# Six edits of one layer kernel: the last tile's splits put first, M6 ahead of M4, adaLN beside V, x loaded first, the last pair kept in SBUF

## The chip, the cores and the metric

The kernel runs on one core of a Trainium2 chip. The metric is the time of one execution on the device in microseconds (us). The engines of the core work side by side and wait for each other by semaphores: PE (TensorE, matrix products), DVE (VectorE), ACT (ScalarE), POOL (GpSimd) and SP (SyncE, which here issues the DMA transfers). PE's clock has two levels, 1.2 and 2.4 GHz; the profile gives the granted clock of a stretch as a share of the higher one.

## The reference, cut to what matters

The kernel computes one hybrid decoder layer over 1024 tokens of 1024 channels.

```
mod = silu(c) @ w_ada + b_ada                     # shift1, scale1, gate1, shift2, scale2, gate2
h = rmsnorm(x, norm1_w) * (1 + scale1) + shift1
proj = h @ w_in                                   # attention q k v, indexer, retention q k v, gates
qr = rotate(qr); kr = rotate(kr) * 128 ** -0.5    # retention keys and queries (4 heads of 128)
att = dsa_attention(...)                          # top-256 by an indexer's score
ret = silu(gr) * groupnorm(retention(qr, kr, vr))
merged = sigmoid(ga) * (att @ w_attn_proj) + sigmoid(gb) * (ret @ w_ret_proj)
x = x + gate1 * (merged @ w_out)
h2 = rmsnorm(x, norm2_w) * (1 + scale2) + shift2
x = x + gate2 * ((silu(h2 @ w_ffn_gate) * (h2 @ w_ffn_up)) @ w_ffn_down)
out = rmsnorm(x, final_norm_w)
```

## The kernel before

Every float32 operand of a large product is **split** into a high and a low part that PE takes (names ending in `hi` and `lo`): ACT copies the operand to `hi`, and POOL or DVE subtracts, `lo = operand - hi`. A product is then three matmuls, hi·hi, hi·lo and lo·hi. `lo_engine` names the engine of the subtraction; `turns_after(a, b)` only sets the order of two instructions on one engine. A scheduler orders the rest, and each engine works its list in order.

The stages, in order of time:

- **Start (0 to 80 us).** SP loads five small rows (`rows`: c, b_ada and norm weights), then the first block of w_ada (`load_wa(0)`), then four tiles of x. For each of eight blocks j, DVE sums `acc` over eight slices of w_ada (L293, L295), PE transposes it, and DVE makes the two columns `modc` (L300, L301). `make_h` (L270) transposes x, ACT writes `hT_hi` and `hx` from PSUM (L277, two instructions), and `lo_engine` makes `hT_lo` (L278: POOL for the first half of the tokens, DVE for the second). Then PE multiplies block j.
- **Rotated retention queries and keys (QR; 231 to 281 us for the first head pair, hp = 0).** Per tile t of eight: PE projects, ACT copies (`qk`, L650), POOL rotates in seven instructions (L657 to L663: `rra`, `rrb`, `rq`, `kk`), PE transposes `rq` and `kk` (L666, L667). Meanwhile DVE runs count passes of the top-k search (L463, `eq`) and steps of `mod_work` (L529, `macc`: the other four sixths of adaLN, 32 steps, each with a load `mw` of 512 KB). A step is called once per t.
- **V and retention (V_R)**, with one step of `mod_work` per t for hp = 0; then attention.
- **Gate region (500 to 715 us).** Products by Strassen's scheme: `Stream` takes 256 columns of a weight in seven products M1 to M7 of half size, whose weight operands are sums of the blocks b11, b12, b21, b22 (`factor`, L762 makes `lo`), and whose results DVE adds up (`add`, L821). The token side (`h11`, `h21`, `S1` to `S4`) is made from `sums` (L625, L638, L639). `seq` is the order of the products, `behind(i)` what else is issued behind product i.
- **FFN start (1110 to 1135 us).** The normalised h2 of the last tile group is transposed, scaled (L1404), split into `hc` (`put_combo`, L1294 and L1295), and the first two streams begin: M1 and M5 early, then M2, M4, M6, M3, M7.
- **FFN streams (1200 to 1540 us).** 22 streams: 11 pairs p of gate and up columns. After a pair, its activations (`act_d`, seven per pair) and the sums of its w_ffn_down blocks (`dw_d`, L1502) go to DRAM.
- **Down product (from 1560 us).** For each of M1, M5, M6, M3, M7, M4 and each p, `down_slot` loads an operand (`draw`, from `act_d`, `dw_d` or w_ffn_down), ACT makes the high part (`dslot`, L1603), DVE or POOL the low one (L1604), and PE multiplies (L1621 to L1623).

Of the kernel before, what the change touches and what calls it, by code (L numbers as in the profile page):

```python
# [43 lines left out]
def tile_hybrid_layer(ctx: ExitStack, tc: tile.TileContext, x, c, w_ada, b_ada, norm1_w, w_in,  # L44
# [202 lines left out]
    rows = start.tile([80, P], F32, name="rows")  # L247
    nc.sync.dma_start(out=rows[0:8, :], in_=c.rearrange("o (k p) -> (o k) p", p=P))
# [4 lines left out]
    load_wa(0)  # L253
    for t in range(4):
        load_x(t)
# [14 lines left out]
    def make_h(j, hf, lo_engine):  # L270
# [5 lines left out]
        for to in (hi, hx):  # L276
            nc.scalar.activation(to, tp, AF.Identity, scale=modc[:, j, 2:3], bias=modc[:, j, 0:1])  # L277
# [7 lines left out]
    def start_mod(j):  # L285
        if j:
            load_wa(j)
# [218 lines left out]
    mod_ins = [None]  # L506

    def mod_work():
# [12 lines left out]
        for n, (m, k) in enumerate(steps):  # L521
# [10 lines left out]
            mod_ins[0] = ins  # L532
# [108 lines left out]
    for hp in range(2):  # L641
# [3 lines left out]
        for t in range(NT):  # L645
# [71 lines left out]
        for t in range(NT + 1):  # L717
# [42 lines left out]
    def split_block(src, hi, lo, eng=None):  # L760
        ins = nc.scalar.activation(hi, src, AF.Copy)  # L761
        (eng or nc.gpsimd).tensor_sub(lo, src, f32(hi))  # L762
        return ins

    class Stream:
# [5 lines left out]
        def __init__(self, env, w, c0):  # L771
# [3 lines left out]
            self.next = None  # L775

        def open(self):
            if self.blocks:
                return
            for kh in range(2):  # L780
# [13 lines left out]
        def factor(self, m):  # L794
# [3 lines left out]
            elif m == "M4":  # L798
                src = self.t2
                nc.vector.tensor_sub(src, b["21"], src)  # L800
            else:
                src = four(self.env.tmp())
                x, y = {"M5": ("12", "11"), "M6": ("22", None), "M7": ("22", "12")}[m]
                if m == "M6" and "M5" in self.early:
                    self.t1 = src
                    nc.vector.tensor_sub(src, b["12"], b["11"])
                nc.vector.tensor_sub(src, b[x], b[y] if y else self.t1)  # L807
# [5 lines left out]
            self.split = split_block(src, hi, lo, self.env.lo_engine)  # L813
# [70 lines left out]
    class GateEnv:  # L884
# [23 lines left out]

        def store(self, st, dst, src):
# [5 lines left out]
        def use(self, st, c):  # L915
# [99 lines left out]
    seq = [(st, m) for m in ORDER for st in flow[:2]]  # L1015
# [6 lines left out]
    def behind(i):  # L1022
        n, m = 2 + (i - 14) // 7, seq[i][1]
        if i == 6:
            genv.lo_engine = None
        if i >= 15 and (i - 15) % 6 == 0 and 22 + (i - 15) // 6 < len(passes) - 1:
            turns_after(passes[22 + (i - 15) // 6], genv.added)
        if 14 <= i < n_mid:
# [3 lines left out]
            if n in (8, 9) and m == "M1":  # L1032
# [723 lines left out]
```

## Time and profile before

| quantity | value |
|---|---|
| median of 3 runs | 1771.59 us (1771.57 to 1774.38) |
| profiled execution, its own time | 1770.31 us |
| its span | 1768.4 us |
| mean granted clock of PE | 0.991 |
| busy share PE, DVE, POOL, ACT | 96%, 69%, 50%, 43% |
| moved by DMA | 266.48 MB, 151 GB/s mean |

The span is the time from the first to the last instruction that the profile shows; the profiled execution took 1.9 us more than that, and 1.3 us less than the median. The stretches named in this document are us from the span's start. A granted clock under 1 means that PE ran at its lower level for part of the stretch.

### The profile page before, as it was taken

What the parts mean: (1) busy time and instruction counts of PE and PEld (TensorE: products, weight loads), DVE (VectorE), ACT (ScalarE), POOL (GpSimd) and SP (SyncE); (2) the same over time, 40 slices, a digit from 0 to 9 for tenths busy, and PEclk for the clock granted to TensorE, in tenths of its full rate; (3) what the DMA queues carried; (4) which work ended last, traced back from release to release, by engine and by line L of the source; (5) the groups of instructions that cost most, each with busy time, mean ns of one, the idle gap of its engine ahead of it and who ended that gap; (6) DMA issues with size and microseconds to landing.
All of it is one profiled execution on the core that took longest, in us unless ns stands there. A gap on an engine that the chain in (4) does not pass through costs nothing. (4 is left out here: it accounts for less than half of the span.)

```text
span 1768.4 us, 24625 instructions
## 1 busy us (share of the span) xinstructions
PE 1696.3 (96%) x8266; PEld 1393.6 (79%) x8266; DVE 1216.7 (69%) x2099; ACT 757.2 (43%) x1469; POOL 882.4 (50%) x873
## 2 busy tenths in 40 slices
PE   5899989999999999999999999899999999999998
PEld 4797768888878887788777888688787778787887
DVE  7529793888998687574675747865756565686665
ACT  3625533333544444430676146533333333444444
POOL 3563275683544678430355631054544445556564
PEclk9999999999999999999999999999999999999999
DMA  9535452512333355964843720134444444597762
GB/s 276 161 99 169 149 162 62 149 39 57 117 90 131 112 172 176 291 182 146 196 116 136 244 98 1 54 107 165 158 156 160 137 150 143 203 320 247 209 183 107
DMA packets 182654, 266.48 MB, mean 151 GB/s; under 512 B 13872, under 2 KB 111616, under 8 KB 180096
## 3 DMA queue, kind: packets, MB, share of 16 engines
q1 hardware_dynamic: 182528, 264.91, 48.1%
q8 instruction: 65, 1.06, 0.3%
q14 instruction: 61, 0.50, 0.1%
HBM read 195.39 MB, written 69.47 MB: 150 GB/s over the span
## 5 line engine op out<-in xcount | busy, mean ns | idle before, releaser
L80 POOL TENSOR_TENSOR wlo<-wraw,whi 128x512 fp32r<-128x512 f32 (+2 forms) x116 | 147.0, 1279 | 105.3 <-ACT whi L77 86.3
L463 DVE TENSOR_SCALAR_CACHE_REDUCE eq<-score,cand 128x384 uint8<-128x384 f32 (+2 forms) x192 | 180.5, 940 | 3.6
L762 POOL TENSOR_TENSOR flo<-tmp,fhi 128x512 fp32r<-128x512 f32 x79 | 107.1, 1356 | 139.7 <-ACT fhi L761 111.8
L121 PE MATMUL mm<-whi,hT_hi 128*128 128x512 f32 (+1 forms) x432 | 159.8, 376 | 3.8 <-ACT qk L650 1.8
L124 PE MATMUL mm<-whi,hT_lo 128*128 128x512 f32 (+1 forms) x432 | 161.5, 376 | 0.0
L123 PE MATMUL mm<-wlo,hT_hi 128*128 128x512 f32 (+1 forms) x432 | 160.3, 374 | 0.0
L838 PE MATMUL ya<-hc,fhi 128*128 128x512 f32 x344 | 134.6, 392 | 2.3 <-DVE c L821 1.4
L1604 DVE TENSOR_TENSOR dslot<-draw,dslot 128x512 fp32r<-128x512 f32 x88 | 94.7, 1107 | 58.4 <-ACT dslot L1603 54.2
L1603 ACT ACTIVATE dslot<-draw 128x512 fp32r<-128x512 f32 x154 | 90.4, 626 | 102.9 <-DMA draw<-dw_d 23.4
L840 PE MATMUL ya<-hc,fhi 128*128 128x512 f32 x344 | 133.9, 389 | 0.0
L842 PE MATMUL ya<-hc,flo 128*128 128x512 f32 x344 | 132.4, 389 | 0.0
L1604 POOL TENSOR_TENSOR dslot<-draw,dslot 128x512 fp32r<-128x512 f32 x66 | 98.0, 1498 | 65.4 <-ACT dslot L1603 61.7
L762 POOL TENSOR_TENSOR flo<-raws,fhi 128x512 fp32r<-128x512 f32 x60 | 82.1, 1369 | 92.7 <-ACT fhi L761 64.2
L77 ACT ACTIVATE whi<-wraw 128x512 fp32r<-128x512 f32 (+2 forms) x116 | 67.0, 590 | 112.0 <-DMA wraw<-in_w_in_dram 46.4
L840 PE MATMUL yb<-hc,fhi 128*128 128x512 f32 x256 | 100.6, 393 | 6.1 <-DVE hc L1295 6.1
L842 PE MATMUL yb<-hc,flo 128*128 128x512 f32 x256 | 100.7, 394 | 3.2 <-POOL flo L762 3.2
L761 ACT ACTIVATE fhi<-tmp 128x512 fp32r<-128x512 f32 x84 | 53.0, 631 | 113.1 <-PE ya L840 61.4
L838 PE MATMUL yb<-hc,fhi 128*128 128x512 f32 x256 | 100.6, 394 | 0.6 <-DVE c L821 0.4
L121 PEld LDWEIGHTS mm<-whi,hT_hi 128*128 128x128 f32 x432 | 80.9, 188 | 16.0 <-ACT qk L650 2.2
L1144 POOL TENSOR_SCALAR sx<-sx,mx 128x128 f32<-128x128 f32 (+7 forms) x64 | 47.8, 752 | 88.0 <-DVE mx L1143 65.1
L124 PEld LDWEIGHTS mm<-whi,hT_lo 128*128 128x128 f32 x432 | 81.3, 189 | 12.7 <-issue 0.5
L807 DVE TENSOR_TENSOR tmp<-raws 128x512 f32<-128x512 f32 x40 | 39.5, 989 | 74.3 <-POOL flo L762 74.3
(410 smaller groups left out, 4950.9 us busy)
## 6 DMA issues: line engine op xcount, KB each, us to landing
draw<-act_d SPq DMA_DIRECT2D x77, 256.0 KB
mw<-in_w_ada_dram SPq DMA_DIRECT2D x32, 512.0 KB
act_d<-c SPq DMA_DIRECT2D x64, 256.0 KB
raw<-in_w_in_dram SPq DMA_DIRECT2D x26, 512.0 KB
raws<-in_w_ffn_gate_dram SPq DMA_DIRECT2D x24, 512.0 KB
raws<-in_w_ffn_up_dram SPq DMA_DIRECT2D x24, 512.0 KB
dw<-in_w_ffn_down_dram SPq DMA_DIRECT2D x22, 512.0 KB
dw_d<-dw SPq DMA_DIRECT2D x11, 1024.0 KB
```

The source lines that it names most:

```text
L77: ins = nc.scalar.activation(hi[:, :n], raw[:, :n], AF.Copy)
L80: nc.gpsimd.tensor_sub(lo[:, :n], raw[:, :n], f32(hi[:, :n]))
L121: ins = nc.tensor.matmul(ps, lhsT=ahi, rhs=whi[:, :n], start=(i == 0), stop=False)
L123: nc.tensor.matmul(ps, lhsT=ahi, rhs=wlo[:, :n], start=False, stop=False)
L124: nc.tensor.matmul(ps, lhsT=alo, rhs=whi[:, :n], start=False, stop=(i == last))
L463: ins = [nc.vector.tensor_scalar(eq[:, :sc.shape[1]], sc, thr[j], None, op0=op, op1=ALU.add, accum_out=cnt[:, j:j + 1]) for j, sc in enume ...
L762: (eng or nc.gpsimd).tensor_sub(lo, src, f32(hi))
L838: mm = nc.tensor.matmul(ps, lhsT=whi[:, k, :], rhs=hhi[:, k, :], start=own and k == 0, stop=False, skip_group_check=True)
L840: nc.tensor.matmul(ps, lhsT=whi[:, k, :], rhs=hlo[:, k, :], start=False, stop=False, skip_group_check=True)
L842: nc.tensor.matmul(ps, lhsT=wlo[:, k, :], rhs=hhi[:, k, :], start=False, stop=k == 3, skip_group_check=True)
L1603: nc.scalar.activation(slot[:, 0], raw, AF.Copy)
L1604: lo_eng.tensor_sub(slot[:, 1], raw, f32(slot[:, 0]))
```

## The change

Six edits; the arithmetic of the large products stays (7840 PE instructions in the lists of both).

1. **Start.** The first tile of x is loaded ahead of `rows`, the other three ahead of w_ada's first block. In `make_h` ACT writes only `hx`; DVE makes `hT_hi` from it by a cast (16 in all).
2. **adaLN.** No steps of `mod_work` in QR; two steps per t instead of one in V_R of hp = 0.
3. **Gate region.** The first two streams run M1, M5, M6, M2, M3, M7, M4; `lo` is made by DVE until product 11 (before: 6) and again in the last two streams; rope loads and stores move.
4. **FFN start.** The last tile's h11 and h21 splits stand ahead of the weight sums; M6 runs ahead of M4; S4 and S3 are split later.
5. **FFN streams.** Each later M4 stands behind the next stream's first product.
6. **Last pair (p = 10).** Its activations and its w_ffn_down sums stay in SBUF: 7 + 1 stores and 7 + 4 loads fewer, most of 256 KB each.

```diff
     rows = start.tile([80, P], F32, name="rows")
+    load_x(0)
     nc.sync.dma_start(out=rows[0:8, :], in_=c.rearrange("o (k p) -> (o k) p", p=P))
...
-    load_wa(0)
-    for t in range(4):
+    for t in range(1, 4):
         load_x(t)
...
-        for to in (hi, hx):
-            nc.scalar.activation(to, tp, AF.Identity, scale=modc[:, j, 2:3], bias=modc[:, j, 0:1])
+        nc.scalar.activation(hx, tp, AF.Identity, scale=modc[:, j, 2:3], bias=modc[:, j, 0:1])
+        nc.vector.tensor_copy(hi, hx)
         lo_engine.tensor_sub(lo, hx, f32(hi))
...
     def start_mod(j):
-        if j:
-            load_wa(j)
+        load_wa(j)
...
-            if hp == 0:
-                next(mgen, None)
-                if t in (2, 4, 6):
-                    turns_after(passes[t // 2], mod_ins[0])
...
-                turns_after(passes[(3, 15)[hp] + t // 2], chunked[0])
+                turns_after(passes[(6, 17)[hp] + t // 2], chunked[0])
             if hp == 0:
-                next(mgen, None)
+                for _ in range(2):
+                    next(mgen, None)
...
-    seq = [(st, m) for m in ORDER for st in flow[:2]]
+    seq = [(st, m) for m in ("M1", "M5", "M6", "M2", "M3", "M7", "M4") for st in flow[:2]]
...
-        if i == 6:
-            genv.lo_engine = None
+        if i in (11, n_mid - 4):
+            genv.lo_engine = None if i == 11 else nc.vector
...
+        def sum_early(self):
+            b = self.blocks
+            self.t1 = b["12"]
+            nc.vector.tensor_sub(self.t1, b["12"], b["11"])
...
+    fenv.behind = [last_h11, last_h21]
...
-    for st, after in zip(flow, (None, {0: 2}, {2: 3}, {0: 3})):
+    for st, after in zip(flow, (None, {0: 2}, {2: 3}, {1: 3})):
...
-    seq = [(st, m) for m in ("M1", "M2", "M4", "M6", "M3", "M7") for st in flow[:2]]
+    seq = [(st, m) for m in ("M1", "M2", "M6", "M4", "M3", "M7") for st in flow[:2]]
...
+    for i in [i for i, (st, m) in enumerate(seq[:-1]) if m == "M4" and i >= n_first]:
+        seq[i:i + 2] = seq[i + 1], seq[i]
...
-        todo.insert(4, lambda: nc.sync.dma_start(out=dw_d[p], in_=dws[p]))
+        if p < NP - 1:
+            todo.insert(4, lambda: nc.sync.dma_start(out=dw_d[p], in_=dws[p]))
...
-        s = down_slot(act_d[p][:, ACT_AT[m], :], nc.vector)
+        here = p == NP - 1
+        s = down_slot(last_act[m] if here else act_d[p][:, ACT_AT[m], :], nc.vector, here=here)
         if m in DW_AT:
+            if here:
+                return s, down_slot(dws[p][:, DW_AT[m], :], nc.gpsimd, here=True)
```

How the lists of DVE change, in three places. The line numbers of the changed kernel differ by a few. First, DVE at the FFN start, from the scaling of the last transposed quarter of h2 (`hraw<-ty,modr`) on. Before:

```order
L1404 TENSOR_SCALAR hraw_10422<-ty,modr 128x128 x4
L806 TENSOR_TENSOR tmp<-raws 128x512 x2
L807 TENSOR_TENSOR tmp<-raws 128x512 x2
L762 TENSOR_TENSOR flo<-raws,fhi 128x512 x2
L807 TENSOR_TENSOR tmp<-raws,tmp 128x512
L1553 TENSOR_TENSOR s_11017<-hraw_10422,hraw_10423 128x512
L807 TENSOR_TENSOR tmp<-raws,tmp 128x512
L1553 TENSOR_TENSOR s_11017<-hraw_10422,hraw_10423 128x512 x2
L1312 TENSOR_TENSOR hraw_10423<-hraw_10423,hraw_10422 128x4x128
L1553 TENSOR_TENSOR s_11017<-hraw_10422,hraw_10423 128x512
L762 TENSOR_TENSOR flo<-raws,fhi 128x512 x2
L1295 TENSOR_TENSOR hc<-hraw_10422,hc 128x4x128 x2
```

After:

```order
L1412 TENSOR_SCALAR hraw_10422<-ty,modr 128x128 x4
L1325 TENSOR_TENSOR hraw_10422<-hraw_10422,hraw_10423 128x4x128
L755 TENSOR_TENSOR flo<-raws,fhi 128x512 x2
L1301 TENSOR_TENSOR hc<-hraw_10422,hc 128x4x128 x2
L1318 TENSOR_TENSOR hraw_10423<-hraw_10423,hraw_10422 128x4x128
L1325 TENSOR_TENSOR hraw_10422<-hraw_10422,hraw_10423 128x4x128
L755 TENSOR_TENSOR flo<-raws,fhi 128x512 x2
```

The splits of the last tile (`hc<-hraw,hc` of 128x4x128) stood behind ten lines (15 instructions) of weight sums (`tmp`), token sums (`s`) and weight splits (`flo`); now they stand behind one difference and two weight splits. Second, DVE in QR of hp = 0, where `eq,cnt` is a count pass over one block of scores and `macc` a step of adaLN. Before:

```order
L527 TENSOR_SCALAR macc<-mw,colT 128x1024
L468 TENSOR_SCALAR rej<-cnt 128x6
L529 SCALAR_TENSOR_TENSOR macc<-mw,colT,macc 128x1024
L477 TENSOR_SCALAR cand<-rej 128x6
L463 TENSOR_SCALAR eq,cnt<-score_768,cand 128x384
L463 TENSOR_SCALAR eq,cnt<-score_769,cand 128x512
L529 SCALAR_TENSOR_TENSOR macc<-mw,colT,macc 128x1024
L463 TENSOR_SCALAR eq,cnt<-score_770,cand 128x640
L565 TENSOR_TENSOR gateb<-gateb,lg 128x512
L529 SCALAR_TENSOR_TENSOR macc<-mw,colT,macc 128x1024
L463 TENSOR_SCALAR eq,cnt<-score_771,cand 128x768
L529 SCALAR_TENSOR_TENSOR macc<-mw,colT,macc 128x1024
```

After:

```order
L467 TENSOR_SCALAR rej<-cnt 128x6
L476 TENSOR_SCALAR cand<-rej 128x6
L462 TENSOR_SCALAR eq,cnt<-score_768,cand 128x384
L462 TENSOR_SCALAR eq,cnt<-score_769,cand 128x512
L462 TENSOR_SCALAR eq,cnt<-score_770,cand 128x640
L462 TENSOR_SCALAR eq,cnt<-score_771,cand 128x768
L462 TENSOR_SCALAR eq,cnt<-score_772,cand 128x896
L462 TENSOR_SCALAR eq,cnt<-score_773,cand 128x1024
```

The steps are gone from between the passes; the first step of this sixth of adaLN now stands 38 rows further down, at the head of V_R. Third, DVE at the start, where `x_t` is the scaling of a tile of x and `acc` the sum over w_ada. Before:

```order
L293 TENSOR_SCALAR acc<-wa,colT 128x256
L295 SCALAR_TENSOR_TENSOR acc<-wa,colT,acc 128x256 x4
L183 TENSOR_SCALAR ms<-ss 128x1
L295 SCALAR_TENSOR_TENSOR acc<-wa,colT,acc 128x256 x2
L236 TENSOR_SCALAR x_t<-x_t,rstd 128x1024
L295 SCALAR_TENSOR_TENSOR acc<-wa,colT,acc 128x256
L183 TENSOR_SCALAR ms<-ss 128x1
L236 TENSOR_SCALAR x_t<-x_t,rstd 128x1024
L183 TENSOR_SCALAR ms<-ss 128x1
L300 TENSOR_TENSOR modc<-tr,colT 128x2
L301 SCALAR_TENSOR_TENSOR modc<-modc,colT 128x1
```

After:

```order
L183 TENSOR_SCALAR ms<-ss 128x1
L236 TENSOR_SCALAR x_t<-x_t,rstd 128x1024
L183 TENSOR_SCALAR ms<-ss 128x1
L236 TENSOR_SCALAR x_t<-x_t,rstd 128x1024
L292 TENSOR_SCALAR acc<-wa,colT 128x256
L294 SCALAR_TENSOR_TENSOR acc<-wa,colT,acc 128x256 x7
L292 TENSOR_SCALAR acc<-wa,colT 128x256
L294 SCALAR_TENSOR_TENSOR acc<-wa,colT,acc 128x256 x2
L299 TENSOR_TENSOR modc<-tr,colT 128x2
L294 SCALAR_TENSOR_TENSOR acc<-wa,colT,acc 128x256
L300 SCALAR_TENSOR_TENSOR modc<-modc,colT 128x1
L294 SCALAR_TENSOR_TENSOR acc<-wa,colT,acc 128x256 x2
L277 CAST hT_hi_119<-hx_220 128x512
```

All four tiles of x are scaled ahead of the first sum, the second sum starts before the first `modc`, and the casts stand between the sums.

## Rows read from the trace of the kernel before

**Rows 1.** the page, busy time of each engine over the whole span
```profile
PE 1696.3 (96%) x8266; PEld 1393.6 (79%) x8266; DVE 1216.7 (69%) x2099; ACT 757.2 (43%) x1469; POOL 882.4 (50%) x873
```

**Rows 2.** windows: stretch, length, busy time per engine (instructions), PEclk, DMA share, GB/s
```profile
2.00:4.00 2.00, 0.16 (x1) 0.18 (x1) 0.00 (x0) 0.00 (x1) 0.00 (x0) 1.00 0.13 33
20.00:60.00 40.00, 30.42 (x137) 23.67 (x138) 37.77 (x72) 18.86 (x33) 20.45 (x19) 1.00 0.85 250
230.00:282.00 52.00, 45.81 (x200) 34.83 (x199) 43.30 (x73) 18.56 (x49) 47.80 (x57) 0.97 0.43 132
300.00:345.00 45.00, 45.00 (x223) 38.35 (x222) 36.94 (x92) 18.23 (x37) 24.37 (x41) 1.00 0.52 148
500.00:530.00 30.00, 25.77 (x105) 20.18 (x104) 30.00 (x40) 14.13 (x24) 20.75 (x11) 0.94 0.34 96
700.00:720.00 20.00, 18.12 (x73) 14.48 (x73) 13.07 (x20) 7.03 (x13) 15.02 (x11) 0.91 0.64 191
1110.00:1135.00 25.00, 17.94 (x75) 14.20 (x74) 24.11 (x45) 15.28 (x31) 0.86 (x1) 0.86 0.13 43
1200.00:1540.00 340.00, 333.86 (x1453) 270.98 (x1452) 205.29 (x224) 125.48 (x216) 165.35 (x122) 1.00 0.46 157
1605.00:1620.00 15.00, 12.54 (x42) 10.09 (x43) 9.39 (x10) 7.21 (x13) 11.58 (x8) 0.77 0.71 233
```

**Rows 3.** what PE waited for, 1110 to 1135: us, times, longest
```profile
PE yb L840 <- DVE hc L1295: 6.1, 1, 6.1
```

**Rows 4.** timeline of DVE, 1112 to 1126: start, us, operation, count
```profile
1114.17 1.36 DVE L1404 TENSOR_SCALAR hraw<-ty,modr 128x128 f32<-128x128 f32 x4 [0.25 <-PE ty L1394]
...
1124.48 1.28 DVE L1295 TENSOR_TENSOR hc<-hraw,hc 128x512 fp32r<-128x512 f32 x2
```

**Rows 5.** what PE waited for, 230 to 282
```profile
PE tr L666 <- POOL rq L663: 3.3, 2, 1.7
...
PE tr L667 <- POOL kk L663: 1.1, 1, 1.1
```

**Rows 6.** groups of instructions of DVE, 230 to 282: count, busy us, mean ns
```profile
L529 DVE SCALAR_TENSOR_TENSOR macc<-mw,colT,macc 128x1024 f32<-128x1024 f32 x8 | 12.7, 1586 | 0.7 <-DMA mw<-in_w_ada_dram 0.5
```

**Rows 7.** timeline of POOL, 231 to 282
```profile
258.14 2.15 POOL L657 TENSOR_TENSOR rra<-qk,cosr 128x512 f32<-128x512 f32 x1
...
264.41 1.30 POOL L657 TENSOR_TENSOR rra<-qk,cosr 128x512 f32<-128x512 f32 x1
...
268.86 1.32 POOL L657 TENSOR_TENSOR rra<-qk,cosr 128x512 f32<-128x512 f32 x1
```

**Rows 8.** what PE waited for, 1600 to 1615
```profile
PE yb L1621 <- ACT dslot L1603: 3.0, 1, 3.0
```

**Rows 9.** what PE waited for, 500 to 530
```profile
PE mm L838 <- ACT hT_hi L638: 3.5, 1, 3.5
```

**Rows 10.** timeline of DVE, 500 to 528
```profile
508.15 1.77 DVE L625 TENSOR_TENSOR sums<-sums,hT_hi 128x512 f32<-128x512 f32 x1
...
516.21 0.68 DVE L625 TENSOR_TENSOR sums<-sums,hT_lo 128x512 f32<-128x512 f32 x1
```

**Rows 11.** what PE waited for, 670 to 720
```profile
PE mm L838 <- DVE sums L821: 1.9, 1, 1.9
```

**Rows 12.** timeline of POOL, 670 to 716
```profile
707.89 7.63 POOL L762 TENSOR_TENSOR wlo<-wraw,whi 128x512 fp32r<-128x512 f32 x5
```

**Rows 13.** what PE waited for, 0 to 80
```profile
PE tr L299 <- DVE acc L295: 9.5, 2, 9.1
```

**Rows 14.** timeline of DVE, 0 to 66
```profile
13.94 0.75 DVE L236 TENSOR_SCALAR x_t<-x_t,rstd 128x1024 f32<-128x1024 f32 x1 [0.67 <-POOL rstd L184]
...
49.67 1.75 DVE L236 TENSOR_SCALAR x_t<-x_t,rstd 128x1024 f32<-128x1024 f32 x1
```

**Rows 15.** what PE waited for, 1200 to 1540
```profile
PE yb L842 <- POOL flo L762: 3.2, 4, 0.8
PE ya L838 <- DVE c L821: 1.4, 4, 0.4
```

More of the change, by code (lines that the diff above doesn't have):

```diff
@@ L774, in __init__ @@
             self.early = ()
-            self.next = None
+            self.next = self.t1 = None
         def open(self):
@@ L798, in factor @@
             elif m == "M4":
-                src = self.t2
-                nc.vector.tensor_sub(src, b["21"], src)
+                src = b["21"] if m in self.early else self.t2
+                self.env.in_turn(None, nc.vector.tensor_sub(src, b["21"], self.t2))
+            elif m == "M7" and "M4" in self.early:
+                src = four(self.env.tmp())
+                self.env.in_turn(None, nc.vector.tensor_sub(src, self.t2, b["11"]))
             else:
@@ L803, in factor @@
                 x, y = {"M5": ("12", "11"), "M6": ("22", None), "M7": ("22", "12")}[m]
-                if m == "M6" and "M5" in self.early:
+                if m == "M6" and "M5" in self.early and not self.t1:
                     self.t1 = src
-                    nc.vector.tensor_sub(src, b["12"], b["11"])
-                nc.vector.tensor_sub(src, b[x], b[y] if y else self.t1)
+                    self.env.in_turn(None, nc.vector.tensor_sub(src, b["12"], b["11"]))
+                self.env.in_turn(None, nc.vector.tensor_sub(src, b[x], b[y] if y else self.t1))
                 if m == "M5":
@@ L812, in factor @@
             hi, lo = self.env.slot()
-            self.split = split_block(src, hi, lo, self.env.lo_engine)
+            self.split, self.lo = split_block(src, hi, lo, self.env.lo_engine)
+            self.env.in_turn(self.split, self.lo)
             return hi, lo
@@ L907, in quad, with in_turn @@
             return quads[(self.n_q - 1) % len(quads)]
+        def in_turn(self, *_):
+            pass
         def store(self, st, dst, src):
@@ L1423, in tile_hybrid_layer, with in_turn @@
         lo_engine = nc.vector
+        behind = []
+        def in_turn(self, scalar, vector):
+            for hi, lo in self.behind:
+                if scalar is not None:
+                    turns_after(scalar, hi)
+                turns_after(vector, lo)
         def __init__(self):
@@ L1477, in finish_tasks @@
                      ("M3", s4)):
-            todo.append(lambda m=m, t=t: act_store(p, m, t))
+            if p < NP - 1:
+                todo.append(lambda m=m, t=t: act_store(p, m, t))
+            else:
+                last_act[m] = t
         if p:
@@ L1559, in behind @@
             fenv.lo_engine = nc.gpsimd
+            fenv.behind = []
         if i == 9:
@@ L1590, in tile_hybrid_layer, with down_slot @@
     n_slot = [0]
-    fnorm = ffn.tile([P, 4, H], F32, name="fnorm", tag="dw")[:, 0:2, :].rearrange("p a n -> p (a n)")
-    nc.sync.dma_start(out=fnorm, in_=final_norm_w.rearrange("(o d) -> o d", o=1).partition_broadcast(P))
-    nc.gpsimd.tensor_scalar(fnorm, fnorm, float(D ** 0.5), 1.0, op0=ALU.mult, op1=ALU.mult)
+    fnorm = [quad_tile("fnorm") for _ in range(2)]
+    for hf, fn in enumerate(fnorm):
+        nc.sync.dma_start(out=fn, in_=final_norm_w[hf * H:(hf + 1) * H].rearrange("(o d) -> o d", o=1)
+                          .partition_broadcast(P))
+        nc.gpsimd.tensor_scalar(fn, fn, float(D ** 0.5), 1.0, op0=ALU.mult, op1=ALU.mult)
     xo_all = slab_tile(7, [P, 8, H], F32, "xo")
-    def down_slot(src, lo_eng, scale=None):
+    def down_slot(src, lo_eng, scale=None, here=False):
         n = n_slot[0]
         n_slot[0] += 1
-        raw, slot = raw_ring[:, n % 8, :], slot_rings[n // 4 % 6][:, n % 4]
-        nc.sync.dma_start(out=raw, in_=src)
+        raw, slot = src if here else raw_ring[:, n % 8, :], slot_rings[n // 4 % 6][:, n % 4]
+        if not here:
+            nc.sync.dma_start(out=raw, in_=src)
         if scale is not None:
@@ L1636, in square @@
             ss3[t] = const.tile([P, 16], F32, name="ss3", bufs=4)
-        sq = ffn.tile([P, H], BF16, name="sqh", tag="quad", bufs=10)
+        if not squares:
+            squares.append(ffn.tile([P, H], BF16, name="sqh", tag="quad", bufs=10))
+        sq = squares[0]
         nc.scalar.activation(sq[:, :c1 - c0], x1[t][:, c0:c1], AF.Square, accum_out=ss3[t][:, i:i + 1])
```

62 lines of the change are left out of this document (35 added, 27 removed).

## Prediction

> **What bounds the kernel now.** The page's first line comes first: PE is busy 96% of the span [rows 1], that is 1696.3 of 1768.4 us, and the change leaves its 7840 listed instructions as they are. So nothing can be won but PE's idle time, 72.1 us, and the time that PE loses at its lower clock. DVE at 69% and POOL at 50% bound nothing on average, but they do in places.
>
> The table of windows shows these places [rows 2]. PE idles 9.6 us of 20 to 60, 6.2 of 230 to 282, 4.2 of 500 to 530, 1.9 of 700 to 720, 7.1 of 1110 to 1135, 6.1 of 1200 to 1540 and 2.5 of 1605 to 1620. A second loss stands beside it: where PE had idled, the granted clock of the window is below 1. Matmuls at the lower level (1.2 instead of 2.4 GHz) take twice as long, so a busy time b at mean clock g could shrink by about b(1 - g): 1.4 us in 230 to 282, 1.5 in 500 to 530, 1.6 in 700 to 720, 2.5 in 1110 to 1135, 2.9 in 1605 to 1620. What PE waits for in each place comes from the views of its waits; what kept that engine, from the timelines. I go through the edits by their size. Below, "bounds" are the two ends that the rows allow.
>
> **FFN start.** PE waits once for 6.1 us, for the low part of the last tile's h11 [rows 3]. On DVE that split starts at 1124.48, behind work that starts with the last scaling at 1114.17 [rows 4]; from the end of the scalings to the split are about 9.0 us, filled with 15 instructions, so 0.60 each. In the changed order the split has three instructions before it (a difference and two weight splits). By the same price it starts at 1115.5 + 3 x 0.60 = 1117.3, and 0.7 us later (the transposes stand three matmuls further back on PE) at 1118.0. Half of its 1.28 for two, 0.64, later the first is done: 1118.6, where before it was 1125.1. PE began to wait at about 1125.1 - 6.1 = 1119.0, so the whole wait goes, with some 0.4 us to spare. What is late next are the 12 instructions that were put back: at 0.60 they are DVE work of 7 us, which M6, the sums S2 to S4 and M4 need only two to eight products later; a product of twelve matmuls takes 12 x 0.23 = 2.8 us (333.86 us for 1453 matmuls is 0.23 each [rows 2]). M6 ahead of M4 costs nothing by itself, since M4's operand needs M6's sum first. With the clock's 2.5, at most 8.6 us are to be had; I take 7.5, since M1's first matmuls may meet another late split. Bounds: -9 and -4.
>
> **Last pair in SBUF.** M5 of the down product waits 3.0 us for a high part of an operand [rows 8], and the window's clock is 0.77, worth 2.9. The operands of p = 10 are stored, and reloaded at once; now ACT can split them where they lie. That also takes 8 stores and 11 loads out of SP's queue. Take -5.0 of 5.9; bounds -6.5 and -1 (if M5 finds the next operand late instead).
>
> **adaLN out of QR.** PE waits 3.3 + 1.1 us for POOL's rotations of hp = 0 [rows 5]; POOL is busy 47.8 of 52 us there [rows 2]. POOL's cycle for one tile, from one L657 to the next, is 264.41 - 258.14 = 6.27 us while steps of adaLN run on DVE, and 268.86 - 264.41 = 4.45 when only count passes do; L657 itself takes 2.15 and 1.30 [rows 7]. PE's own need is 45.81/8 = 5.7 us a tile [rows 2], between the two: with the steps POOL is too slow, without them it has 1.3 us to spare. So the 4.4 goes; of the clock's 1.4 I take little, since the stage's other idle time, 6.2 - 4.4 = 1.8 us, stays: -4.5. Bounds: -5.8, and -1 if something else in that stage slows POOL. The eight steps, 1.59 us each [rows 6], go to V_R: 12.7 us more for DVE in a stretch where it is busy 36.9 of 45 and PE is never idle [rows 2]. Seven of these fit into DVE's 8.1 us of idle; the rest is covered by count passes, which no product of this stage waits for and which move back. If that cover is gone, V_R's masks come late by up to 12.7 - 8.1 = 4.6 us; that is in the rivals.
>
> **Gate region, both ends.** In 500 to 530 PE waits 3.5 us for S3's high part [rows 9], which stands behind the sums on DVE. A sum takes 1.77 us beside POOL's weight splits and 0.68 alone [rows 10]. Now DVE does five more splits itself (5 x 0.60 = 3.0 us more) but four or five sums cost 1.1 less each (4.4 to 5.5), and two products, 5.5 us, stand ahead of M3 on PE. Take -3.5, the wait alone; bounds -6 and 0. In 700 to 720 PE waits 1.9 us for a sum on DVE [rows 11], which stood behind DVE work waiting for POOL, and POOL was working through five weight splits in 7.63 us [rows 12]. DVE, busy 13.07 of 20 us there [rows 2], now makes these. Take -2.5 of 1.9 + 1.6; bounds -4.5 and 0. A page speaks against both: the Trainium skill (Perfetto Trace Analysis, Optimizing Scalar/DVE Operations) says that POOL and DVE share an SBUF read port, so that moving work between these two might not help. By it both terms would be 0, and the sum 6 us less. The traces bear the sharing out, 1.77 against 0.68, but the moved split has then no partner on POOL to share with, so I keep the terms.
>
> **Start.** PE first waits for the sum of w_ada's block [rows 13]. DMA moved next to nothing from 2 to 4 us (share 0.13 [rows 2]), since only small rows were asked for; with a tile of x first, loads begin up to 2 us sooner. From 20 to 60 DVE is busy 37.77 of 40 us, so it is the bound there, and the casts add eight instructions to it. No row has one. Half of an L236 alone (128x1024, 0.75) gives 0.4; half of one beside POOL, 1.75 [rows 14], gives 0.9, so the eight cost 3 to 7 us. Against this, ACT's second pass per block is saved, the first block's sum isn't interrupted by scalings, and the second sum starts before the first `modc`. The other eight casts come with the second half of the tokens, after the sums. I take -2; bounds -6 and +5.
>
> **FFN streams.** PE waits 3.2 us in four pieces for POOL's splits and 1.4 in four for DVE's additions [rows 15]; only the second kind is what M4's place changes. Take -1; bounds -6 and +3.
>
> **The sum.** -7.5 - 5.0 - 4.5 - 3.5 - 2.5 - 2 - 1 = -26.0. From the profiled execution's 1770.31 that is 1744.3; the median of the runs is 1.28 higher, so I forecast 1745.6. The bounds add up to -43.8 and +2; as they are independent, their half-widths (2.5, 2.8, 2.4, 3, 2.3, 5.5, 4.5) combine to about 9.3.
>
> **The rivals.** *The port moves only change places:* the gate's two terms and the streams' come to nothing, 7 us less: 1752.6. For it speaks that DVE is busy all 30 us of 500 to 530 [rows 2]; against it, that the same sums took 0.68 when POOL was quiet.
>
> *V_R takes back what QR gave:* the masks come late by 4.6 us and the start's casts cost their 7 instead of being hidden (+5 for -2): 11.6 less, 1757.2. For it speaks DVE's 82% in 300 to 345; against it, that count passes can wait.
>
> *The casts fight POOL at the start.* L236, with one input, took 1.75 beside POOL against 0.75 alone [rows 14]. A wait of 1.0 for each of 8 casts and for POOL's 8 splits would be 16 us on the bound chain, less 2 for the earlier loads: with the other 24 us it leaves 1771.6 - 24 + 14 = 1761.6. The Trainium skill (SBUF — State Buffer, Who interferes with whom) says that a copy or cast on DVE can run in a mode that takes both ports, and that it or POOL then waits for the whole of the other's instruction. By that page this rival would be the rule; no row has a cast, and the nearest one, L236, agrees with the page.
>
> *Slower: the streams.* Each later M4 now stands behind the next stream's first product. If that product isn't ready, PE waits for its split, once for each of 20 streams. A POOL split takes 1.5 us in company (7.63/5 [rows 12]), so 30 us, +4 net of the other 25: 1776. It decides from 1.4 us per stream. Against it: POOL is busy 165 of 340 us there, so splits can be early, and the worst of such waits now is 0.8.
>
> **How the numbers follow.** The forecast 60%, the first rival 18%, the second 10%, the third 6%, slower 4%, and 2% for a balance at no change. The range reaches from 1736 (9.3 below) to 1760, so as to hold the first two rivals; the forecast's own is 1736 to 1755. A measurement can tell about 0.2%, 3.5 us, from no change: faster 0.93, same 0.03, slower 0.04.
>
> **What would show it.** In the changed profile: no wait on `hc` at 1110 to 1135 and clock 1.00 there; no wait of L666 or L667 but the first in QR, with POOL's cycle near 4.5; no wait on `dslot` when M5 reaches p = 10; at most 1 us left at each end of the gate region; the first block's matmuls no later than 20.7 us and the last block's `acc` no later than 64. Wrong would be the forecast if V_R or the streams show new waits, if casts take over 1 us each, or if waits taken away at one place appear as waits at the next product.

## The result and the profile after

The changed kernel takes 1746.66 us (median of 4 runs, 1744.10 to 1747.54) against 1771.74 for the kernel before in the same comparison: a ratio of 0.9853, 95% interval 0.9836 to 0.987, or 25.1 us less. The forecast was 1745.6. Its profiled execution took 1747.43 us, with a span of 1745.7.

The windows of the changed kernel, cut like [rows 2], with one at the head of V_R (282 to 300) and one where M5 of the down product now reaches p = 10 (1583 to 1598). Columns: stretch, length, busy time of PE, PEld, DVE, ACT and POOL (instructions), granted clock of PE, DMA share, GB/s.

```profile
20.00:60.00 40.00, 34.48 (x151) 26.62 (x150) 38.41 (x75) 14.03 (x25) 22.32 (x20) 1.00 0.74 242
230.00:282.00 52.00, 49.61 (x220) 39.42 (x219) 49.76 (x88) 17.39 (x48) 43.52 (x61) 0.97 0.18 51
282.00:300.00 18.00, 12.13 (x50) 9.87 (x51) 14.86 (x23) 3.08 (x6) 3.58 (x5) 0.91 0.79 248
300.00:345.00 45.00, 45.00 (x219) 38.27 (x218) 33.23 (x91) 17.41 (x34) 21.67 (x37) 1.00 0.38 116
500.00:530.00 30.00, 29.52 (x130) 23.92 (x130) 30.00 (x48) 15.45 (x26) 8.24 (x5) 1.00 0.29 88
700.00:720.00 20.00, 20.00 (x89) 16.50 (x89) 14.82 (x22) 9.59 (x18) 2.42 (x2) 1.00 0.63 201
1110.00:1135.00 25.00, 24.44 (x114) 19.98 (x113) 23.99 (x44) 19.34 (x38) 0.00 (x0) 1.00 0.12 37
1200.00:1540.00 340.00, 338.00 (x1490) 279.24 (x1489) 213.16 (x233) 128.63 (x225) 179.22 (x127) 1.00 0.48 163
1583.00:1598.00 15.00, 15.00 (x68) 12.42 (x67) 12.10 (x12) 9.87 (x17) 11.55 (x8) 1.00 0.79 262
```

PE's idle time is gone from 500 to 530, 700 to 720, 1110 to 1135, most of 1200 to 1540, and the down product. It stands now where before there was none: 5.9 of 18 us at the head of V_R, at a clock of 0.91.

A better table than that of idle time is where each stage ends. For each stage this is the start of the last row of its kind in PE's two timelines (a row can stand for several instructions in a line), and the shift from one stage to the next is what the stage gained or lost:

| stage (its last row of PE) | before | after | stage's own shift | forecast |
|---|---|---|---|---|
| start and indexer (`lg<-klo,qst`) | 231.52 | 229.75 | -1.8 | -2 |
| QR and V_R, first pair (`tr<-qkT`) | 339.26 | 340.52 | +3.0 | -4.5 |
| QR and V_R, second pair (`tr<-qkT`) | 449.41 | 454.37 | +3.7 | 0 |
| gate region (up to the first `tra` of attention) | 848.28 | 848.42 | -4.8 | -6 |
| attention, output product, transposes of h2 (`ty`) | 1113.07 | 1113.12 | -0.1 | 0 |
| FFN start and streams (last product with `hc`) | 1552.67 | 1535.24 | -17.5 | -8.5 |
| down product (last with `dslot`) | 1761.60 | 1738.65 | -5.5 | -5 |

The sum is -23.0, near the -26.0 of the forecast, but the table is far off in opposite directions: QR and V_R of the two head pairs lost 6.7 us instead of gaining 4.5, and the FFN gained 9 us more than I said. The experiments are mostly about these two.

One caution on such a table: it compares single executions. The start, for one, ended between 228.25 and 231.73 in the eight other profiles below that have the changed start as it stands. So between runs the length of a stage tells more than the time at which it ends.

What PE waited for in the changed kernel, 230 to 300 (us in total, times, longest), against [rows 5]:

```profile
PE tr L673 <- DVE inn L675: 4.1, 1, 4.1
PE mm L121 <- ACT qk L646: 1.8, 1, 1.8
PE tr L662 <- POOL rq L659: 1.5, 1, 1.5
PE tr L663 <- POOL kk L659: 0.9, 1, 0.9
```

The three waits for rotations within QR are gone, as forecast. The two that are left come at 283 and 284, with V_R already begun, and a new one of 4.1 us for a mask (`inn`) follows at 294. DVE's timeline ahead of them (start, us, operation, shape, count) shows something that the profile of before has nowhere:

```profile
265.70 1.28 DVE L462 TENSOR_SCALAR_CACHE_REDUCE eq<-score,cand 128x1024 uint8<-128x1024 f32 x1
267.02 7.20 DVE L467 TENSOR_SCALAR rej<-cnt 128x6 int32<-128x6 f32 x1
274.25 0.17 DVE L482 SCALAR_TENSOR_TENSOR cand<-cand,rej 128x6 int32<-128x6 int32 x1
...
275.90 0.69 DVE L561 TENSOR_TENSOR gateb<-gateb,lg 128x512 f32<-128x512 f32 x1
```

`rej<-cnt` compares six numbers per partition. In the profile of before it takes 0.14 to 1.28 us; here it took 7.20. POOL's timeline in the same stretch has no gap:

```profile
266.95 1.28 POOL L80 TENSOR_TENSOR wlo<-wraw,whi 128x512 fp32r<-128x512 f32 x1
268.18 0.47 POOL L659 TENSOR_TENSOR rq<-rra,rrb 128x128 f32<-128x128 f32 x1
268.59 0.47 POOL L659 TENSOR_TENSOR kk<-rra,rrb 128x128 f32<-128x128 f32 x1
269.01 2.55 POOL L80 TENSOR_TENSOR wlo<-wraw,whi 128x512 fp32r<-128x512 f32 x2
271.51 1.30 POOL L653 TENSOR_TENSOR rra<-qk,cosr 128x512 f32<-128x512 f32 x1
272.75 0.74 POOL L654 TENSOR_TENSOR rrb<-qk,sinr 128x256 f32<-128x256 f32 x1
273.45 0.74 POOL L655 TENSOR_TENSOR rrb<-qk,sinr 128x256 f32<-128x256 f32 x1
```

POOL's row ends at 273.45 + 0.74 = 274.19, DVE's comparison at 267.02 + 7.20 = 274.22. The same happens in the second pair, at 401.76 for 5.87 us. I call this the stall. Behind it on DVE stands the addition of a gate's bias (L561, at 275.90), and SP's queue has a store of its result in its list. SP's wait at that store, 266 to 300:

```profile
SPq L562 <- DVE gateb L561: 8.0, 1, 8.0
```

Weights of V and blocks of w_ada stand behind that store in SP's list. Not all of the 8.0 is the stall's: SP waited at this store for 3.0 us in a run without the stall (two passes on ACT, below), so it delayed these loads by some 5 us.

The second pair shows a limit of this reading. PE's waits there, 345 to 375, come before the stall at 401.76, and the profile of before has none in the second pair:

```profile
PE tr L662 <- POOL rq L659: 1.2, 1, 1.2
PE lg L688 <- ACT on L697: 0.7, 1, 0.7
PE tr L662 <- DVE modr L547: 0.4, 1, 0.4
```

At the FFN start the changed DVE list did what its order said; the timeline against [rows 4]:

```profile
1114.19 1.37 DVE L1412 TENSOR_SCALAR hraw<-ty,modr 128x128 f32<-128x128 f32 x4
1115.48 0.68 DVE L1325 TENSOR_TENSOR hraw<-hraw,hraw 128x512 f32<-128x512 f32 x1
1116.08 1.29 DVE L755 TENSOR_TENSOR flo<-raws,fhi 128x512 fp32r<-128x512 f32 x2
1117.28 1.29 DVE L1301 TENSOR_TENSOR hc<-hraw,hc 128x512 fp32r<-128x512 f32 x2
```

The last tile's split starts at 1117.28 instead of 1124.48, and PE's wait of 6.1 is one of 0.6 in the same stretch:

```profile
PE ya L842 <- DVE hc L1301: 0.6, 1, 0.6
```

Both kernels end their last transposes at the same time. By 1140 us PE had done 144 matmuls with `hc` in the changed kernel and 109 in the one before: 35 more, at 0.227 us each 7.9 us.

### The profile page after: what moved, and what is told of

Read it like the earlier page. It is cut to its first block, busy times and chain, and to the rows that moved or that the text cites. A ratio compares the mean times of both kernels' runs of the same rounds, so it can differ in the third digit from the quotient of the medians.

```text
span 1745.7 us, 24593 instructions
## 1 busy us (share of the span) xinstructions
PE 1688.6 (97%) x8266; PEld 1393.6 (80%) x8266; DVE 1239.8 (71%) x2134; ACT 746.5 (43%) x1454; POOL 856.7 (49%) x855
## 3 DMA queue, kind: packets, MB, share of 16 engines
q8 instruction: 65, 1.06, 0.3%
## 4 chain that ended last, share of the span: by engine, by line
PE 72%; DVE 15%; issue 4%; DMA 4%; POOL 3%; ACT 1%; SPq 0%; POOLq 0%; DVEq 0%; ACTq 0%
DVE eq L462 5%; PE ya L842 4%; PE ya L840 4%; PE ya L844 4%; PE yb L840 3%; PE yb L842 3%; PE yb L844 3%; PE ya L1663 2%; PE ya L1661 2%; PE ya L1662 2%; PE pva L1182 2%; DVE acc L294 2%; PE tra L1161 2%; PE mm L124 2%; PE mm L121 2%
## 5 line engine op out<-in xcount | busy, mean ns | idle before, releaser
L1640 ACT ACTIVATE dslot<-draw 128x512 fp32r<-128x512 f32 x143 | 85.0, 628 | 96.1 <-DMA draw<-act_d 24.7
L755 POOL TENSOR_TENSOR flo<-raws,fhi 128x512 fp32r<-128x512 f32 x60 | 86.4, 1446 | 73.7 <-ACT fhi L754 38.7
L1641 DVE TENSOR_TENSOR dslot<-draw,dslot 128x512 fp32r<-128x512 f32 x81 | 88.9, 1129 | 47.2 <-ACT dslot L1640 46.9
L808 DVE TENSOR_TENSOR tmp<-raws 128x512 f32<-128x512 f32 x40 | 30.6, 768 | 87.0 <-POOL flo L755 87.0
```

Source lines behind the costliest of these rows:

```text
L755: return ins, (eng or nc.gpsimd).tensor_sub(lo, src, f32(hi))
L1640: nc.scalar.activation(slot[:, 0], raw, AF.Copy)
L1641: lo_eng.tensor_sub(slot[:, 1], raw, f32(slot[:, 0]))
```

## The experiments

Ratios are to the kernel before on the same chip. They have intervals of 0.13% to 0.21% either way (2.3 to 3.7 us); so where two variants are compared, the ends of the stages in their profiles are told too, by the rows of the table above.

**The streams' swap alone.** The kernel before, with:

```diff
+    for i in [i for i, (st, m) in enumerate(seq[:-1]) if m == "M4" and i >= n_first]:
+        seq[i:i + 2] = seq[i + 1], seq[i]
```

> The kernel before with one edit: each later M4 stands behind the next stream's first product. Theory 1 (the streams' waits cost about twice what the view of PE's waits shows, since each break of the row of matmuls also costs a restart, and this edit alone removes them): 1762 us, 10 less than before, and PE's spacing at 1200 to 1540 without breaks. Rival (the prediction's step: only DVE's additions, 1.4 us, are touched by it; the rest came from the new FFN start): 1770 to 1771 us.

It took 1759.18 us against 1769.12: 0.9939 (0.9919 to 0.996). Its executions spread more than the others (1752.56 to 1764.19), and the profiled one took 1754.66. In that one the FFN ended 11.56 us earlier than before's, of which 1.65 were there at the last transposes, so FFN start and streams gained 9.9; the down product, with no edit there, gained 4.4 more. The rival, 1770 to 1771, falls, and theory 1 holds as to the size. PE's waits from 1200 to 1540 in this run:

```profile
PE ya L838 <- DVE c L821: 2.0, 2, 1.6
```

POOL's four waits are gone, and what is left is for DVE's additions, the kind that the prediction said the swap would touch. The window of this run for 1200 to 1540, against [rows 2], shows the rest of the gain:

```profile
1200.00:1540.00 340.00, 338.01 (x1491) 279.27 (x1490) 214.94 (x233) 128.85 (x224) 178.82 (x128) 1.00 0.47 164
```

PE did 1491 matmuls instead of 1453 in these 340 us: 38 more, at 0.227 us each 8.6 us, where the idle time shrank by only 338.01 - 333.86 = 4.2. The rest was hidden in "busy". PE's timeline of before around one wait (start, us, operation) shows how:

```profile
1294.36 0.39 PE L838 MATMUL yb<-hc,fhi 128*128 128x512 f32 x1
1294.59 0.39 PE L840 MATMUL yb<-hc,fhi 128*128 128x512 f32 x1
1295.77 0.50 PE L842 MATMUL yb<-hc,flo 128*128 128x512 f32 x1 [0.80 <-POOL flo L762]
1296.11 0.39 PE L838 MATMUL yb<-hc,fhi 128*128 128x512 f32 x1
```

Matmuls start every 0.23 us but last 0.39, so they overlap. At the wait the starts are 1.18 and 0.34 apart instead of 0.23: 0.95 + 0.11 = 1.06 us lost, of which the view of waits counts 0.80. Over 1140 to 1540 before has 34 spacings above 0.245 us; by this sum they cost 10.8 us, against 6.1 us of idle time in 13 waits. So most of the late starts are too short for the view to list. This run has 4 such spacings, which cost 2.5 us.

**adaLN's move alone.** The kernel before, with no steps in QR, two per t in V_R, and the count passes paced as in the change:

```diff
-            if hp == 0:
-                next(mgen, None)
...
-                next(mgen, None)
+                for _ in range(2):
+                    next(mgen, None)
```

> The kernel before with one edit: no steps of adaLN in QR, two per t in V_R, and the count passes paced as in the changed kernel. Theory 1 (V_R loses more than QR gains): 1774 to 1777 us, with waits of the masks' transposes at the head of V_R. Rival (the prediction's step; the loss in V_R comes from another edit): 1767 us, no such wait.

1770.97 against 1769.12: 1.0019 (1.0001 to 1.0037). Slower by 0.2 to 6.5 us, less than theory 1 said, but on its side. (Its executions took 1767.78 to 1784.6, the profiled one 1774.43.) The head of V_R shows the new wait:

```profile
PE tr L674 <- DVE inn L676: 4.1, 1, 4.1
```

But there is no stall in this run. The comparison at the same place, beside the same row of POOL (58 instructions, 7.2 us of them still to come), took 0.41 us:

```profile
271.40 0.41 DVE L468 TENSOR_SCALAR rej<-cnt 128x6 int32<-128x6 f32 x1
```

So the masks are late by 4.1 us even without the stall: the move alone does that, with steps that wait for their loads ahead of the masks in DVE's list. The first pair took 106.6 us here against 107.7 before, and the second 113.5 against 110.2.

**The change without adaLN's move.** The reverse of that edit, on the changed kernel.

> The changed kernel with the adaLN edit undone: one step per t in QR and in V_R. Theory 1: 1741 to 1743 us, 4 to 6 less than the changed kernel, with 4.4 us of waits for POOL's rotations back in QR and none for the masks. Rival (the prediction's step): 1751 us, 4.5 more.

1743.84 against 1769.12: 0.985 (0.9836 to 0.9864), where the changed kernel has 0.9853 and, in a later comparison, 0.9869. By ratio it is no slower, and perhaps 0 to 3 us faster, so the prediction's 4.5 us fall. Its first pair took 106.9 us and its second 110.6, against 110.8 and 113.9 in the changed kernel. QR has its waits back, and V_R none for a mask:

```profile
PE tr L665 <- POOL rq L662: 4.8, 3, 1.9
PE mm L121 <- ACT qk L649: 1.8, 1, 1.8
```

In the second pair the comparison stood 5.87 us here, and 5.85 in the run with the swap alone. Neither has adaLN's move. So the stall of the second pair doesn't come from the move, and it cost these two runs little: their second pair took 110.6 and 111.0 us, against 110.2 without a stall.

**The comparison with two inputs.** If the stall hung on the form of the instruction, another form should end it:

```diff
-            nc.vector.tensor_scalar(rej, cnt, float(TOPK), float(value), op0=ALU.is_lt, op1=ALU.mult)
+            nc.vector.scalar_tensor_tensor(rej, cnt, float(TOPK), powers[:, b, :], op0=ALU.is_lt, op1=ALU.mult)
```

> The changed kernel with the tiny comparison of the top-k search (L467, 128x6) written with two inputs, the second a table of powers of two; same values, same place. Theory 2 (that comparison stood still for 7.2 us at 267 and 5.9 us at 402 while POOL ran instructions back to back, DVE's additions of the gate bias came late behind it, SP's queue stood 8 us at the store that waits for them, and the weights and adaLN's blocks behind that store came late for V_R): the comparison takes under 1.5 us everywhere, SP's wait at that store falls to about 1 us, the waits at the head of both V_R stages fall by 4 to 7 us, 1740 to 1743 us. Rival (two steps per t with two buffers for adaLN's blocks are slow by themselves, since each waits for a load): 1745 to 1747 us, the masks' wait of 4 us stays.

1750.38 against 1769.12: 0.9888 (0.9874 to 0.9903), slower than the changed kernel. The stall stayed, 7.22 us instead of 7.20:

```profile
269.35 7.22 DVE L471 SCALAR_TENSOR_TENSOR rej<-cnt,powers 128x6 int32<-128x6 f32 x1
```

So this run couldn't tell theory 2 from its rival; it shows that the stall doesn't hang on that form. Its start ended 2.4 us and its gate region took 2.5 us more than the changed kernel's; the first has 32 new instructions of POOL that fill the table, but the cause of neither is shown.

**adaLN's steps behind the masks.** On the changed kernel:

```diff
                 for _ in range(2):
                     next(mgen, None)
+                    turns_after(mod_ins[0], mask_ins[0])
```

> The changed kernel, each adaLN step of V_R ordered on DVE behind the last mask product (L675) issued before it. Theory 3 (the masks came late because six steps, each waiting for its load, stood ahead of the first mask in DVE's list): no wait of the masks' transposes over 0.5 us at the head of the first V_R, so 4 to 6 us less than the changed kernel, a ratio to before of 0.982. Rival (the two steps per t ask for more loads than DMA and SP's queue give there, wherever DVE does them): the wait moves to the next stage (POOL's weight splits or the second QR), ratio 0.985 or more.

1740.88 against 1770.27: 0.9835 (0.9816 to 0.9854). Theory 3's mark, no wait for a mask, is not met:

```profile
PE tr L676 <- DVE inn L678: 4.2, 1, 4.2
```

No step of adaLN stands ahead of the first masks any more, but the comparison stood still for 9.47 us, and the masks behind it in DVE's list came late by that:

```profile
266.85 9.47 DVE L467 TENSOR_SCALAR rej<-cnt 128x6 int32<-128x6 f32 x1
...
289.25 0.29 DVE L678 TENSOR_TENSOR inn<-tr,rmask 128x128 f32<-128x128 f32 x1
```

From the comparison's end at 276.32 to that mask DVE has no gap. The first pair took 111.9 us, the changed kernel's 110.8; what this run gained, 4.8 us, came in the gate region, for a reason that the runs don't show.

**V's low parts on DVE.** The other cause alone: on the changed kernel, POOL's row is opened by giving eight weight splits per head pair to DVE.

```diff
+        lo_eng[0] = nc.vector
         slots = [rows_slot([(w_in, C_VR + 2 * DV * hp, 2 * DV)], k) for k in range(KT)]
+        lo_eng[0] = nc.gpsimd
```

> The changed kernel with the eight low parts of V's weights in each head pair made by DVE instead of POOL, so that POOL's row of instructions at the end of QR has gaps. Theory 4 (two causes, each enough by itself for the masks' wait: the tiny comparison stands as long as POOL runs without a gap, and adaLN's steps stand ahead of the first masks): the comparison takes under 1.5 us, but the masks' wait of 3 to 4 us stays because of the steps; 0 to 3 us less than the changed kernel. Rival (the stall is the one cause): no masks' wait, 5 us less.

1737.33 against 1769.79: 0.9811 (0.9797 to 0.9824), where the changed kernel in the same comparison has 0.9869 (0.9856 to 0.9883). That is 10.3 us less by the medians, three times what theory 4 allowed and twice what the rival did. The comparison takes at most 1.27 us anywhere, and the masks' waits, 2.2 us in all, are half as long:

```profile
PE tr L676 <- DVE inn L678: 2.2, 2, 1.8
PE mm L122 <- ACT qk L647: 1.8, 1, 1.8
```

The first pair took 100.7 us instead of 110.8, the second 117.4 instead of 113.9, and the gate region 5.1 us less. This edit does more than end the stall: it also takes eight splits per pair off POOL, so its whole gain is not the stall's price. Neither theory 4 nor the rival said this.

**Both.** V's low parts on DVE, and the steps behind the masks.

> The changed kernel with both: V's low parts on DVE, and each adaLN step of V_R behind the last mask before it. Theory 4: comparison under 1.5 us and no masks' wait over 1 us at the head of the first V_R; the end of V_R 4 to 6 us earlier than in the changed kernel, ratio to before 0.981 to 0.983. Rival (the two steps per t ask for more loads than the queue gives): the masks' wait stays or turns into a wait for V's weights.

1739.98 against 1769.79: 0.9828 (0.9815 to 0.9842). No wait for a mask is left:

```profile
PE mm L122 <- ACT qk L650: 1.8, 1, 1.8
PE mm L122 <- ACT whi L78: 0.4, 1, 0.4
```

Its first pair took 101.8 us, 1.1 more than in the run before, though a wait of 2.2 us is gone, and the two ratios' intervals overlap. The theory's statement on the masks holds (with both causes gone, the wait is); that the order behind the masks gains time is not shown.

**No move of adaLN, and V's low parts on DVE.**

> The changed kernel with the adaLN edit undone, and V's low parts on DVE. Theory 4: QR keeps its three waits for POOL's rotations (4 to 5 us), V_R has none, the comparison takes under 1.5 us also in the second QR; as fast as the changed kernel without the adaLN edit or up to 2 us faster, ratio 0.983 to 0.985. Rival (POOL's relief also ends the rotations' waits): QR's waits under 2 us, ratio 0.981 to 0.982.

1737.76 against 1769.79: 0.9817 (0.9804 to 0.9831), the same as with the move. QR's waits for POOL stay, 3.2 us in two. Against the change without the move (0.985) the splits bring some 6 us even here, where the first pair had no stall to lose: its first pair took 103.5 us, 3.4 less than in that run, and its gate region 5.4 less, while the second pair took 4.3 more.

**The changed kernel again.**

> The changed kernel itself, as the yardstick for the other three on the same chip: ratio to before 0.984 to 0.987, and a profile that shows how far one execution's gate region and V_R differ from another's.

1747.6 against 1769.79: 0.9869 (0.9856 to 0.9883). Its comparison stood 7.24 and 5.89 us, its masks' wait was 4.5, its first pair took 112.2 us (1.4 more than in the first profile), its second 114.3, and its gate region the same 394.0.

**Two passes on ACT.** The changed kernel with ACT writing `hT_hi` and `hx` as before, no casts.

```diff
-        nc.vector.tensor_copy(hi, hx)
+        for to in (hi, hx):
+            nc.scalar.activation(to, tp, AF.Identity, scale=modc[:, j, 2:3], bias=modc[:, j, 0:1])
```

> The changed kernel without the casts on DVE: ACT makes the high part from PSUM again, as before. The prediction's step (the eight casts cost about what the saved pass of ACT gives): within 2 us of the changed kernel, ratio 0.984 to 0.986. Rival (the casts take turns with POOL at the start and cost 1 us or more each on the engine that is the bound there): 6 to 10 us less, ratio 0.980 to 0.982.

1742.24 against 1770.27: 0.9844 (0.9827 to 0.9862), as the prediction's step said. The indexer ended at 231.24, 1.5 and 0.9 us later than in the two profiles with casts, so no cost of the casts shows. A cast, which no row of before had, is in the changed kernel's groups of DVE for 0 to 60:

```profile
L277 DVE CAST hT_hi<-hx 128x512 fp32r<-128x512 f32 x6 | 2.5, 422 | 0.0
```

0.42 us is half of what L236 takes alone [rows 14]; the lower bound. In this run the order of the two engines fell otherwise at 267, by chance, and the comparison didn't stand still there (only in the second pair, 5.86 us):

```profile
268.60 0.43 DVE L467 TENSOR_SCALAR rej<-cnt 128x6 int32<-128x6 f32 x1
```

The edit doesn't touch the first pair, so this is the changed kernel without the first stall. The first pair took 104.5 us: 6.3 less than in the changed kernel, and 3.2 less than before the change. The second pair took 114.1, as in the changed kernel. The masks' wait was 1.8.

**The gate's splits on POOL.** The changed kernel with the old rule.

```diff
-        if i in (11, n_mid - 4):
-            genv.lo_engine = None if i == 11 else nc.vector
+        if i == 6:
+            genv.lo_engine = None
```

> The changed kernel with the gate region's low parts made by POOL as before (DVE only up to product 6, none in the last two streams). The prediction's step (the moved splits and the order of M2 bring 6 us): 2.5 to 6 us more than the changed kernel, ratio 0.9867 to 0.9885, with a wait near 700 for a sum of DVE. Rival (POOL and DVE share their way to memory, so the move brings nothing; the gain there is M2's place alone): ratio 0.985.

1749.83 against 1770.27: 0.9889 (0.987 to 0.9907). The gate region (end of V_R to the first `tra`) took 397.0 us instead of 394.0, so the move of splits is worth 3.0; the rest of the 4.8, by subtraction, lies in M2's place and the rope's. The cost came back at the region's head, at 525.69, as a wait for DVE's sum:

```profile
PE lg L840 <- DVE kept L823: 1.6, 1, 1.6
```

The rest of the region ran as in the changed kernel: from the 500th PE instruction of the region on this run is 2.9 us behind and stays so. So the splits of the last two streams, which this run gave back too, were worth nothing. The Trainium skill (Perfetto Trace Analysis, Optimizing Scalar/DVE Operations) says that moving work between POOL and DVE might not help; at the region's head it did, at its end it didn't.

**The last pair through DRAM.** The changed kernel with p = 10 stored and loaded again.

> The changed kernel with the last pair's activations and w_ffn_down sums stored and loaded again, as before. The prediction's step (keeping them in SBUF brings 5 us): 4 to 6 us more than the changed kernel, ratio 0.9875 to 0.989, a wait of 3 us for an operand of p = 10 at M5. Rival (the streams' swap alone took most of that wait away, as in the run with the swap alone, where it shrank to 0.6 us): 0 to 1 us more, ratio 0.985 to 0.986.

1743.98 against 1770.27: 0.9857 (0.984 to 0.9873), inside the changed kernel's own interval. So by the time of the whole, keeping the pair in SBUF shows no gain. By its profile the down product took 205.7 us from the end of the streams, 2.3 more than the changed kernel's 203.4 and 3.2 less than before's 208.9; the wait at M5 was half of what it was before:

```profile
PE yb L1657 <- ACT dslot L1636: 1.6, 1, 1.6
```

## Why the prediction was right in its sum and wrong in several terms

- **FFN start (-7.5): right.** FFN start and streams gained 17.5 together and the swap alone 9.9, so 7.6 are left for the start; counted by matmuls it is 7.9. The split's start, worked out as 1118.0, was 1117.28.
- **FFN streams (-1, bounds -6 and +3): mis-sized; the term measured -9.9,** outside its own bounds. The step that failed is "only the second kind is what M4's place changes": the swap ended POOL's four waits, and waits for DVE stayed. And the base was too small, since a wait as the view counts it is less than what it costs: 6.1 us of waits from 1140 to 1540, 10.8 by the spacing of matmuls. Why the swap ended POOL's waits is not shown.
- **adaLN out of QR (-4.5): wrong in sign; the two pairs lost 6.7.** The price of the rotations was right: the waits within QR went, and came back in the run without the move (4.8). What failed is the sentence that count passes cover the moved steps. (Its count was off too: at 1.59 us each, five of the eight steps fit into 8.1 us, not seven.) Three things came in its place.
  - The moved steps stand in one list with the masks, and made them late: by 4.1 us in the run with adaLN's move alone, where nothing stalled. That is the rival "V_R takes back what QR gave", with its price of 4.6.
  - The stall of the first pair, which no rival had, cost some 6 us. The run that missed the stall by chance took 104.5 in the first pair, the four profiles that have the stall and the same edits there 108.6 to 112.2, and the changed kernel's own 110.8: 4.1 to 7.7 less, and 6.3. A second way to the price agrees: V's low parts on DVE shortened the first pair by 10.0 us where there was a stall and by 3.4 where there was none, a difference of 6.6.
  - The second pair lost 3.7. It took 112.7 to 114.3 us in every run with the move and V's splits on POOL, and 110.2 to 111.0 in the three without the move, with and without a stall there. So this goes with the move and not with the stall; by which wait is not shown.
  
  Without the first stall the move gains 1 to 3 us in the first pair and loses 3 to 4 in the second, so it is worth nothing here: with V's splits on DVE the kernels with and without the move take the same time.
- **Last pair in SBUF (-5.0): the place right, the cause half.** The stage gained 5.5, but the swap alone gained 4.4 there, and keeping the pair in SBUF adds 1.1 (against the swap alone) to 2.3 (against the run through DRAM), which the time of the whole doesn't show. The two edits take away the same wait, and I gave it to one.
- **Gate region (-6): -4.8, and its two halves missed.** Counted in PE instructions from the region's start, the changed kernel was 5.8 us ahead by the 300th, where the forecast for the head was -3.5. From there to the region's end it lost 1.0, where the forecast for the end was -2.5: the wait for the sum went, but a new one of 2.2 us for a high part of ACT stands at 696, with a clock of 0.67 from 695 to 700. The rival that moves between POOL and DVE only change places fell at the head and held at the end.
- **Start (-2): -1.8, by luck as far as the runs show.** The loads began earlier (DMA's share from 2 to 4 us is 0.87 instead of 0.13), but nothing came of it: the first block's matmuls came at 22.50 (20.67 before; the mark was 20.7), PE waited 12.9 us for the first `acc`, and the last block's `acc` ended at 66.0 (64.3 before). By 80 us PE had done 237 instructions, and 239 before. The gain came from 80 to 100 (149 instructions against 137), where no step of the prediction stands, and it is smaller than the spread of the start between profiles. The casts cost 0.42 each, and the rival of casts against POOL fell.
- **Slower by the streams:** fell; the opposite happened.

The first paragraph's step to the clock doesn't hold everywhere either: "where PE had idled, the granted clock of the window is below 1" is not so for 20 to 60 and 1200 to 1540, where [rows 2] have 1.00. No term was priced from these two. Two sums are off by little: the half-widths combine to 9.2 instead of 9.3, and 30 us less the other 25 are +5, so the slower rival stands at 1776.6.

That the sum came out near is luck to the extent that -9 and +11 cancelled.

## What to carry to other kernels

Price a wait of PE by the distance between the starts of its matmuls, not by the idle time alone: short waits before cost nearly twice what was listed. An instruction that nothing waits for is no cover if something that is waited for stands behind it in the same list. Look in the timeline for single instructions that took many times what the same one takes elsewhere; a group's mean hides them. And before a loss is put down to such a one, look whether it is there in runs with the loss, and missing in those without: of two stalls here, one cost some 6 us and the other next to nothing.

## What the runs showed of the hardware

A DVE instruction of 128x6 that starts beside one of POOL's rotations or splits mostly ends 0.03 us or a little more behind it: in the changed kernel at 246.05 and 252.98, where POOL's ended at 246.02 and 252.95. The Trainium skill (SBUF — State Buffer, SBUF: two separate sides) says that the shared pair of ports is held for one whole instruction and the other engine waits, and these cases agree. But in 9 of the 14 profiles such a comparison, with one tensor input or with two, stood still once or twice until POOL's whole row of back-to-back instructions had ended: 7.20 and 5.87 us in the changed kernel, 7.22 with two inputs, 9.47 at the most. It then ended 0.02 or 0.03 us behind the row each time. In the first of these, eight instructions of POOL passed, so the wait can last much longer than one instruction.

An unbroken row of POOL is not enough for it. In the first pair before, POOL's row is unbroken from 233.73 to 287.56, and the four comparisons beside it took 0.18 to 1.26 us; with adaLN's move alone the one with 7.2 us of the row to come took 0.41. What decides whether POOL's next instruction goes first is not shown. The count passes beside the same row weren't slowed (1.28 at 265.70, as alone).
